# A two-layer diffusion trunk on one core: the seams between ten stages of one kernel are reordered

## The chip, the cores and the metric

The kernel runs on one core of one Trainium2 chip. The metric is the device time of one execution in microseconds (us). The engines of a core are TensorE (PE in the profile; its weight loads are shown apart as PEld), VectorE (DVE), ScalarE (ACT), GpSimd (POOL) and SyncE (SP, which here only issues transfers). Each engine works through its own queue in order, and semaphores make one wait for another. A measured time is the median of several executions; a profiled execution is a single one, with its trace.

## The reference

A trunk of two layers works on 1024 latent tokens and 256 context tokens of width 1024. Every layer modulates its input with a shift and a scale that come from a condition vector, mixes tokens by attention, adds the gated result to the input and normalises it; then it does the same with a feed-forward that has a convolution over three tokens inside. Cut to what matters:

```python
for l in range(DEPTH):                       # 2 layers
    m_lat = split6(silu(c) @ ada_w[l] + ada_b[l])        # shift, scale, gate, twice
    m_ctx = split6(silu(c_ctx) @ ada_w[l] + ada_b[l])
    h_lat, h_ctx = modulate(x_lat, m_lat[0], m_lat[1]), modulate(x_ctx, m_ctx[0], m_ctx[1])
    if l % 2 == 0:   # heads A: global attention, 8 query and 2 key heads, RMS norm and rotary
                     # heads B: neighbourhood attention on a 16x64 grid, 8 heads, learned bias
        y_lat, y_ctx = even_mixer(h_lat, h_ctx, ...)
    else:            # windowed attention (+-128 tokens), 16 query and 2 key heads, sink logits
        y_lat, y_ctx = odd_mixer(h_lat, h_ctx, ...)
    x_lat = layer_norm(ALPHA * x_lat + m_lat[2] * y_lat)
    x_lat = layer_norm(ALPHA * x_lat + m_lat[5] * conv_ffn(modulate(x_lat, m_lat[3], m_lat[4])))
    # layer 0 does the same two steps for x_ctx; layer 1 only uses the context's keys and values
```

`conv_ffn` is `u = h @ w_up` (1024 to 5632), a three-tap convolution along tokens, `silu(g) * a` of the two halves, and `@ w_down` (2816 to 1024). Every latent or context query sees the context keys; all is in 32-bit floats.

## The kernel before

**Precision.** A matrix product is made of three passes: an operand is split into a high part, cast by ACT, and a low part, the difference, made by DVE or POOL, and high x high, low x high and high x low are summed in PSUM (`mm3`, lines 429 to 431; `product`, L1860). So every weight that is loaded costs a cast (L112 or L1832) and a difference (L113 or L1834). In the feed-forwards of the latent tokens the 2x2 blocks of a product are combined with seven multiplications instead of eight; the sums of weight blocks are made on DVE (L1836, L1839; they are called ("s", i) in the code), and the sums of input blocks, T0 to T3, are stored to DRAM (`dT`) and loaded back in `load_T` (hi by ACT, L1889; lo by DVE, L1890).

**Stages in order.** `l0_project` (layer 0's modulated input, query, key and value products, token tile by token tile; then the features of heads B), `attn_ab` (global attention in groups of one token tile and one key head, then neighbourhood attention), `l0_out` (output product, residual, norm), `ffn` (context feed-forward), `ffn2` (latent feed-forward), `l1_project`, `attn_c`, `l1_out`, `ffn7` (latent feed-forward of layer 1). Both output products go through `out_project`.

**What sets the order.** Each engine's order is normally found by a planner from priorities and estimated readiness. In the attention stages and in later parts of `l0_project` the order of TensorE is written by hand (`manual_pe`); in `l1_project` that of TensorE and DVE; in `ffn`, `ffn2` and `ffn7` that of all engines. `out_project` is left to the planner. SP's queue issues most loads, and an issue that waits for something holds back all that stand behind it.

**The places that matter here.**

- *Modulation sums.* `ada_items` walks over the modulation weights still missing in layer 0, in eight jobs of seven steps: loads of `araw`, DVE multiply-adds into `acc` (L228, the first product of a column L224), the split of the result (ACT L325, DVE L326), and a sum over partitions by two matmuls with ones into a PSUM bank `small` (L330, L331), followed by an add on DVE (L332). The matmuls wait in `self.pend` until some tiles have passed. `bg(n)` in `l0_project` advances n steps after each token tile or feature chunk. Steps left over run out in one piece after the second feature product.
- *Global attention.* `groups_a` gives a list of groups (key head, token tile); tiles 8 and 9 are the context. A group's scores (matmul L910) go through a row pass on DVE (L1156 for latent keys, L1173 for context keys: negate and take the minimum), an exponential on ACT (L933), a reciprocal on DVE (L935) and a scaling on POOL (L936); then they are transposed (L1043) and multiplied with the values (L1057). `pipeline` takes units as tuples whose second number says how many slots ahead the scores are issued. `mod_late` (L367 to L370) turns modulation rows into coefficients, at two groups of this stage.
- *Neighbourhood attention.* `slices_b`; the context unit has its scores and its row passes (L1289) for two token tiles in one loop.
- *Output product.* `out_project` loads, for each token tile, x, then y; y is split by ACT (L1457) and POOL (L1458). The first tile's y is ready from before.
- *Context feed-forward.* `ffn` begins with the broadcast of the gate (L159), then the first row of down weights (`row(0)`, L1611). Up weights of part f + 2 are loaded at part f.
- *Latent feed-forward of layer 1.* `build_B1` makes the last token tile's input and the sums; `ffn7` then loads T0 and T1, and after their use T2 and T3 into the same buffers. Each part multiplies W1 with T0 into V, later W4 with T1 into Y, then W5 with T2 into Q (read by L2498, through a copy L2480).
- *Second projection.* `l1_project` scales rows of x by the norm's gain and adds its bias (`scale_rows`, L2627 and L2628), a tile at a time.
- *Windowed attention.* `attn_c`; the row pass is L2887, with a maximum `nm`. At eight of its groups `x_load` fetches a row block of x and scales it with `scale_rows` on DVE.

## Time and profile before

| | before |
|---|---|
| times of three runs | 2835.11, 2832.03, 2835.51 us (median 2835.11) |
| profiled execution | 2826.76 us, span 2825.0 us |
| mean granted clock of TensorE | 0.993 of full speed |
| TensorE busy | 2739.5 us, 97% of the span |
| DVE, ACT, POOL busy | 2155.0 (76%), 1380.8 (49%), 641.9 us (23%) |
| HBM traffic | 161 GB/s over the span |

The profile comes from one execution. A row of waits names the instruction that waited, what released it, and then the total us, how often, and the longest. A row of a timeline has start, duration, engine, line, operation and operands, and in brackets the idle time before it with its releaser. In a window's row the busy time and number of instructions of each engine stand behind the length of the window, then the clock granted to TensorE, the busy share of the DMA engines and the GB/s moved. Matmuls overlap, so the duration of one is longer than its pace.

### The profile page before, as it was taken

To read this page: it belongs to the slowest core of one execution; us is meant where nothing else is said; L and a number is where in the kernel's file an instruction comes from. 1 tells how busy PE (TensorE), PEld (TensorE's weight loads), DVE (VectorE), ACT (ScalarE), POOL (GpSimd) and SP (SyncE) were. 2 spreads that over 40 slices of the span, in tenths; PEclk is the share of its full clock that TensorE was granted. 3 is DMA by queue.
4 is the path that set the end of the run, shared out by engine and by line. 5 is a ranking of instruction groups with operands and counts; after the bars stand their busy time and mean duration, and the time that the engine had idled before them with its cause. 6 is when DMAs were issued, how large, how long until landed. Compare 5 with 4: busy or idle time off the path is not lost.

```text
span 2825.0 us, 45395 instructions
## 1 busy us (share of the span) xinstructions
PE 2739.5 (97%) x16724; PEld 2244.3 (79%) x16724; DVE 2155.0 (76%) x3887; ACT 1380.8 (49%) x2596; POOL 641.9 (23%) x933
## 2 busy tenths in 40 slices
PE   8999899999999999999999999999999999999998
PEld 6887677877788978888888888866678788888887
DVE  4756777776688778888888656677778888888878
ACT  4321355577336645555553345266654555455542
POOL 3601233355440000000001002255543011111002
PEclk9999999999999999999999999999999999999999
DMA  7668601042549653433358525662235455555962
GB/s 272 192 193 284 217 26 35 11 163 91 183 131 275 198 158 110 123 109 117 114 205 291 176 97 165 186 183 90 89 112 168 146 179 175 167 174 200 342 229 97
DMA packets 369350, 457.02 MB, mean 162 GB/s; under 512 B 26008, under 2 KB 265016, under 8 KB 367592
## 3 DMA queue, kind: packets, MB, share of 16 engines
q1 hardware_dynamic: 341512, 369.27, 41.0%
q0 software_dynamic: 24576, 82.89, 8.5%
q8 instruction: 131, 2.15, 0.3%
q10 hardware_dynamic: 3040, 1.97, 0.2%
q14 instruction: 91, 0.75, 0.1%
HBM read 338.11 MB, written 115.93 MB: 161 GB/s over the span
## 4 chain that ended last, share of the span: by engine, by line
PE 74%; issue 9%; DVE 7%; DMA 3%; ACT 3%; POOL 2%; SPq 0%; ACTq 0%; DVEq 0%; POOLq 0%
PE q L1860 8%; PE x L1860 8%; PE y L1860 8%; PE S L910 4%; PE v L1860 4%; PE dy L2544 4%; PE mm L429 4%; PE mm L431 4%; PE mm L430 4%; PE T L1043 3%; PE pv L1057 3%; PE dx L2544 3%; PE d L431 3%; PE d L429 3%; PE d L430 3%
## 5 line engine op out<-in xcount | busy, mean ns | idle before, releaser
L936 POOL TENSOR_SCALAR P<-P,rin 128x640 f32<-128x640 f32 (+3 forms) x288 | 251.1, 877 | 312.6 <-DVE rin L935 285.3
L1834 DVE TENSOR_TENSOR w<-raw,w 128x512 fp32r<-128x512 f32 x308 | 209.9, 695 | 84.3 <-ACT w L1832 84.2
L112 ACT CAST w<-raw 128x512 fp32r<-128x512 f32 x315 | 183.3, 620 | 163.9 <-PE d L431 67.1
L113 DVE TENSOR_TENSOR w<-raw,w 128x512 fp32r<-128x512 f32 x315 | 207.9, 701 | 71.3 <-ACT w L112 69.3
L910 PE MATMUL S<-k,q 64*128 64x256 f32 (+2 forms) x1824 | 199.1, 338 | 20.6 <-DVE nm L2887 8.8
L933 ACT ACTIVATE P<-P,nm 128x641 f32<-128x641 f32 (+4 forms) x208 | 161.5, 778 | 86.8 <-DVE nm L2887 46.0
L1832 ACT CAST w<-raw 128x512 fp32r<-128x512 f32 x308 | 182.2, 620 | 17.2 <-DVE raw L1839 7.5
L910 PEld LDWEIGHTS S<-k,q 64*128 64x128 f32 x1824 | 138.9, 188 | 60.3 <-issue 15.3
L1043 PE MATMUL T<-ident,P 128*128 128x128 f32 x1008 | 133.9, 281 | 5.4 <-POOL P L936 4.9
L429 PE MATMUL d<-w,w 128*128 128x512 f32 x352 | 137.5, 391 | 0.0
L431 PE MATMUL d<-w,w 128*128 128x512 f32 x352 | 137.0, 389 | 0.0
L430 PE MATMUL d<-w,w 128*128 128x512 f32 x352 | 137.0, 389 | 0.0
L1057 PE MATMUL pv<-PT,v 128*64 128x128 f32 x2016 | 131.0, 278 | 4.6 <-ACT PT L923 2.4
L1057 PEld LDWEIGHTS pv<-PT,v 128*64 128x64 f32 x2016 | 108.8, 137 | 28.2 <-issue 13.1
L1043 PEld LDWEIGHTS T<-ident,P 128*128 128x128 f32 x1008 | 109.5, 142 | 24.4 <-issue 14.5
L935 DVE RECIPROCAL rin<-den 128x1 f32<-128x1 f32 x288 | 46.0, 161 | 100.7 <-ACT P L933 97.7
L1860 PE MATMUL q<-T3h,w 128*128 128x512 f32 x352 | 117.1, 394 | 5.7 <-DVE ug L2092 3.1
L2544 PE MATMUL dy<-w,w 128*128 128x512 f32 x528 | 120.8, 390 | 0.2 <-DVE w L113 0.2
L1860 PE MATMUL q<-T2h,w 128*128 128x512 f32 x352 | 115.9, 390 | 2.1 <-ACT q L2480 1.7
L933 ACT ACTIVATE P<-P,mc 128x1280 f32<-128x1280 f32 (+1 forms) x80 | 94.7, 1189 | 44.1 <-DVE mc L1178 41.9
L2544 PEld LDWEIGHTS dy<-w,w 128*128 128x128 f32 x528 | 98.9, 188 | 21.6 <-DVE w L113 0.6
L1860 PE MATMUL v<-T0h,w 128*128 128x512 f32 x352 | 115.5, 389 | 0.0
(465 smaller groups left out, 7786.4 us busy)
## 6 DMA issues: line engine op xcount, KB each, us to landing
raw<-in_up_dram SPq DMA_DIRECT2D x132, 512.0 KB
raw<-in_down_dram SPq DMA_DIRECT2D x59, 512.0 KB
raw<-g SPq DMA_DIRECT2D x44, 512.0 KB
raw<-G SPq DMA_DIRECT2D x38, 512.0 KB
araw<-in_ada_w_dram SPq DMA_DIRECT2D x32, 512.0 KB
raw<-in_w_in_dram SPq DMA_DIRECT2D x28, 512.0 KB
g<-cv POOLq DMA_DIRECT2D x22, 512.0 KB, 3.0
G<-go POOLq DMA_DIRECT2D x44, 256.0 KB, 3.0
```

What stands on the lines that cost most here:

```text
L113: (lo_eng or nc.vector).tensor_sub(lo, s, f32(hi))
L429: nc.tensor.matmul(ps, lh, rh, start=first, stop=False)
L430: nc.tensor.matmul(ps, lh, rl, start=False, stop=False)
L431: nc.tensor.matmul(ps, ll, rh, start=False, stop=last)
L910: self.nc.tensor.matmul(outs[a], q[r, x, qs], k[r, y, ks], start=(i == 0), stop=(i == 2))
L933: nc.scalar.activation(P[:, :m], P[:, :m], AF.Exp, bias=negm, scale=-1.0, accum_out=den)
L936: nc.gpsimd.tensor_scalar(P[:, :n], P[:, :n], rin, 1.0, ALU.mult, ALU.mult)
L1043: nc.tensor.transpose(ps[:, s * 128 : (s + 1) * 128], P[a][:, cols[i + x] : cols[i + x] + 128], self.ident,)
L1057: nc.tensor.matmul(O[a * HD : (a + 1) * HD], v_of(a, vts[i + x]), pT[:, s * 128 : (s + 1) * 128], start=(i + x == 0), stop=(i + x == m - 1 ...
L1834: nc.vector.tensor_sub(half(i, 1), src[i], f32(half(i, 0)))
L1860: nc.tensor.matmul(ps, w[:, a, s], r[b][:, k], start=first and k + i == 0, stop=k == 3 and i == 2, skip_group_check=True,)
L2544: nc.tensor.matmul(banks[q][t], ga[i][:, a, c], wd[i][:, b], start=q < 2 and f + k == 0, stop=f == HF - 1 and k == 2, skip_group_check=True,)
```

## The change

It has ten parts, all of order or placement, in the order of the kernel's stages.

1. The PSUM pool of the modulation sums has two banks instead of one; a pending sum is issued one tile earlier, and more steps are issued per tile.
2. In the global attention a latent group stands between the two context groups; the four heads of a context group share one tile P, and its scores are issued two slots ahead instead of seven.
3. The modulation coefficients made in that stage go from DVE to POOL.
4. The context unit of the neighbourhood attention issues all its scores ahead of its row passes.
5. `out_project` issues the load of the second tile's y ahead of the gate and of x.
6. The first down row and the up weights of part 3 are loaded in the stage before `ffn`, and the row is split there; the gate's broadcast moves into part 4.
7. The weight sum ("s", 1) of the first part of `ffn2` is made at the end of `ffn`.
8. In `ffn7` all four T are staged at once, T1 first, in other buffers; for three of them the first low part is made by POOL, and so is one low part in `build_B1`. Parts with products made ahead take T1's product in front of T0's.
9. `l1_project` scales rows one tile ahead.
10. In `attn_c` the multiply stands behind the row pass of a group's first unit, the add behind the second's.

Two tiles named "pad", 128 bytes per partition each, go. The core of the diff:

```diff
@@ mod_late
+        eng = eng or nc.vector
-                nc.vector.tensor_scalar(s1, ct[:, o + 8 : o + 16], 1.0, None, ALU.add)
-                nc.vector.tensor_mul(ab[:, 0], ct[:, 0:8], s1)
...
+                eng.tensor_scalar(s1, ct[:, o + 8 : o + 16], 1.0, 1.0, ALU.add, ALU.mult)
+                eng.tensor_mul(ab[:, 0], ct[:, 0:8], s1)
...
@@ l0_project
-            if self.pend and self.pend[0][0] > 2:
+            if self.pend and self.pend[0][0] > 1:
...
-                bg(1 if t < 2 else 2)
+                bg(2 if t < 1 else 3)
...
-            banks[0] = e3.enter_context(self.pool("paf", bufs=1, space=PSUM))
+            banks[0] = e3.enter_context(self.pool("paf", bufs=2, space=PSUM))
...
-                    bg(0 if scale and len(n_ev) > 10 else 2 if n > 256 else 1)
+                    bg(0 if scale and len(n_ev) > 10 else 2)
@@ groups_a
-                    for _ in range(4):
-                        P.append(self.t(Pp, [128, TALL], "P"))
+                    if t < NLAT:
+                        P += [self.t(Pp, [128, TALL], "P") for _ in range(4)]
+                    else:
+                        r = self.t(Pp, [128, TALL], "P")
+                        P += [r[:, h * 256 : h * 256 + 256] for h in range(4)]
...
-                        return [(ctx_part, 7, lambda: banks(0) + banks(1), 4, 1)]
+                        return [(ctx_part, 2, lambda: banks(0) + banks(1), 4, 1)]
...
-                group(kv, t, t == NLAT) for kv in range(2) for t in [8, 9] + list(range(NLAT))
+                group(kv, t, t == NLAT) for kv in range(2) for t in [8, 0, 9] + list(range(1, NLAT))
@@ slices_b, context unit, behind the two qk_pair calls
+                for i, x in enumerate(gs):
+                    c = slice(256 + i * 256, 512 + i * 256)
@@ out_project
+        def load_y(t):
+            ys[t] = yh, yl = [self.t(st, [128, KT, 128], n, R, bufs=2) for n in ("yh", "yl")]
+            for q in range(2):
+                s = slice(4 * q, 4 * q + 4)
+                nc.sync.dma_start(f32(yl[:, s]), yv[:, s, t * 128 : (t + 1) * 128])
+
+        load_y(order[1])
         gate_of(order[0])
@@ l0_out, where the first up parts are made
+                r = self.t(self.raw, [128, D], "raw")
+                nc.sync.dma_start(r, io["down"][0][:128])
+                W["r"] = self.up_raws(0, 3)
                 W["u"] = {f: self.ctx_up(pu, W[f], h2c) for f in range(2)}
+                W["d"] = self.split([r[:, :512], r[:, 512:]], 512)
@@ ffn
-            self.bcast(gate, gate_row)
...
-            row(0)
...
                 if f == 4:
+                    self.bcast(gate, gate_row)
...
-            self.early = (part, raws[NP + 1])
+            self.early = (part, self.up_parts(raws[NP + 1]))
+            self.early[1][1]("s", 1)
@@ build_B1
-            nc.vector.tensor_sub(l, s, f32(h))
+            (nc.gpsimd if t == NLAT - 1 else nc.vector).tensor_sub(l, s, f32(h))
@@ ffn7 (staging buffers and load_T changed to fit)
+                for i in range(2):
+                    for m in (1, 0, 2, 3):
+                        make[m].load(i)
...
+                for m in (1, 0, 2, 3):
+                    make[m](0, eng=nc.gpsimd if m != 1 else None)
+                    make[m](1, 2)
...
+                    def first():
+                        self.product(W[1], T[0], V, True)
+                        nc.scalar.copy(u1, cols(V))
+
+                    def second():
+                        self.product(W[4], T[1], Y, False)
+                        nc.scalar.copy(Q, Y)
+
+                    two = (second, first) if p in pre else (first, second)
+                    two[0]()
...
+                    two[1]()
@@ l1_project
-                        load_rows(t + 1)
-                        self.scale_rows(*xs.pop(t), gb["ln_g"], gb["ln_b"])
+                        for u in (0, 1) if t == 0 else (t + 1,):
+                            load_rows(u + 1)
+                            if u < NLAT:
+                                self.scale_rows(*xs.pop(u), gb["ln_g"], gb["ln_b"])
@@ attn_c
-                self.scale_rows(*xs[t], *gb)
+
+            def behind(scores, f):
+                def g():
+                    a, b = scores()
+                    return [
+                        a[:2] + (lambda: (a[2](), f(0))[0],) + a[3:],
+                        b[:2] + (lambda: (b[2](), f(1))[0],) + b[3:],
+                    ]
+                return g
+
+            def x_scale(t, i):
+                x, dr = xs[t]
+                if i == 0:
+                    nc.vector.tensor_mul(x, x, gb[0])
+                else:
+                    nc.vector.tensor_add(x, x, gb[1])
+                    nc.gpsimd.dma_start(dr, x)
...
+                for t, g in enumerate(xg):
+                    gl[g] = gl[g][0], behind(gl[g][1], lambda i, t=t: x_scale(t, i))
```

More of the change, by code (lines that the diff above doesn't have):

```diff
@@ L350, in ada_sum, with mod_late @@
         nc.sync.dma_start(self.d["ada"][l, v, part : part + 1, o : o + W], br)
-    def mod_late(self, tp, pp, lg, lb, mods, tag, bufs=1, bank="small"):
+    def mod_late(self, tp, pp, lg, lb, mods, tag, bufs=1, bank="small", eng=None):
         nc = self.nc
+        eng = eng or nc.vector
         rows = [self.row128(lg), self.row128(lb)]
@@ L1095, in mods @@
                         sp, pt, io["ln_g"][0, i], io["ln_b"][0, i],
-                        [(a[l, v, p], a[l, v, p + 1]) for v in range(2)], tag, 2, "T",
+                        [(a[l, v, p], a[l, v, p + 1]) for v in range(2)], tag, 2, "T", nc.gpsimd,
                     ))
@@ L1451, in out_project @@
             else:
-                yh, yl = (self.t(st, [128, KT, 128], n, R, bufs=2) for n in ("yh", "yl"))
+                if t not in ys:
+                    load_y(t)
+                yh, yl = ys.pop(t)
                 for q in range(2):
@@ L1863, in product, with load_T @@
                 )
-    def load_T(self, tp, stage, dT, m, off):
+    def load_T(self, tp, stage, dT, m, off, late=False):
         nc = self.nc
@@ L1880, in rows, with load, make @@
             return r[:, a - c * n // 2 : b - c * n // 2]
-        for x in part[: 2 if J == 128 else 3]:
-            nc.sync.dma_start(rows(*x), dT[m, :, x[1] : x[2]])
-        def make(*which):
+        def load(i):
+            nc.sync.dma_start(rows(*part[i]), dT[m, :, part[i][1] : part[i][2]])
+        for i in () if late else range(2 if J == 128 else 3):
+            load(i)
+        def make(*which, eng=None):
             for i in which:
@@ L1889, in make @@
                 nc.scalar.copy(hv, r)
-                nc.vector.tensor_sub(lv, r, f32(hv))
+                (eng or nc.vector).tensor_sub(lv, r, f32(hv))
+        make.load = load
         return (h, lo), make
@@ L2038, in ffn2 @@
                         call = lambda what, i: i in (0, 2) or call0(what, i)
+                    elif p == 0:
+                        W2, call0 = raws
+                        call = lambda what, i: (what, i) == ("s", 1) or call0(what, i)
                     elif p + 1 < NP:
@@ L2407, in get_T @@
                 if m in more:
-                    T[m], make[m] = self.load_T(tp, stage(m), dT, m, 0)
+                    T[m], make[m] = self.load_T(tp, stage(m), dT, m, 0, True)
             def make_T(m, *which):
@@ L2428, in ffn7 @@
                 for m in range(4):
-                    if m == 2 and 0 in make:
-                        make_T(0)
-                        make_T(1)
                     get_T(m)
-                    for p in pre if m == 1 else []:
-                        Q = self.t(pu, [128, 512], f"q{p}")
-                        YQ[p] = early["x", p], early["y", p], Q
-                        adds(Q)
+                for i in range(2):
+                    for m in (1, 0, 2, 3):
+                        make[m].load(i)
+                for p in pre:
+                    Q = self.t(pu, [128, 512], f"q{p}")
+                    YQ[p] = early["x", p], early["y", p], Q
+                    adds(Q)
+                for m in (1, 0, 2, 3):
+                    make[m](0, eng=nc.gpsimd if m != 1 else None)
+                    make[m](1, 2)
                 for p in range(NP):
```

47 lines of the change are left out of this document (23 added, 24 removed).

## The prediction

> **What bounds the kernel now.** The first view is the table of busy time by engine.
>
> ```profile
> PE 2739.5 (97%) x16724; PEld 2244.3 (79%) x16724; DVE 2155.0 (76%) x3887; ACT 1380.8 (49%) x2596; POOL 641.9 (23%) x933
> ```
>
> TensorE is busy for 97% of a span of 2825.0 us, so all its waits together are 85.5 us, and nothing but these, or the speed at which it runs, can be won without taking work from it. The change takes no matrix work away. So the second view is TensorE's waits, asked for each seam apart; the rows stand with the steps below. The third is its granted clock, in windows laid over every place where it falls between start-up and the last microseconds; each row has the stretch, its length, the busy time of TensorE, its weight loads, VectorE (DVE), ScalarE (ACT) and GpSimd (POOL), then the clock.
>
> ```profile
> 225.70:232.50 6.80, 4.91 (x38) 3.78 (x36) 3.94 (x7) 0.60 (x1) 0.53 (x1) 1.00 0.89 303
> 232.50:239.30 6.80, 6.47 (x20) 4.09 (x21) 6.66 (x12) 1.41 (x3) 0.53 (x1) 0.50 0.89 288
> 324.70:328.10 3.40, 3.30 (x20) 2.92 (x20) 0.00 (x0) 1.17 (x2) 0.89 (x2) 0.50 0.26 71
> 570.50:573.90 3.40, 3.40 (x26) 3.07 (x23) 1.12 (x5) 1.06 (x4) 1.87 (x5) 0.50 0.34 145
> 853.80:860.60 6.80, 4.74 (x11) 3.43 (x12) 5.05 (x11) 4.40 (x9) 0.77 (x1) 0.50 1.09 345
> 1051.80:1055.20 3.40, 2.86 (x7) 2.31 (x8) 3.37 (x7) 0.00 (x0) 0.00 (x0) 0.51 0.00 0
> 1840.20:1850.40 10.20, 8.96 (x44) 6.87 (x46) 6.31 (x18) 6.07 (x15) 4.05 (x9) 0.50 0.95 321
> ```
>
> The first row is a stretch at full clock for comparison; the six others run at 0.50. At half clock the busy time is twice what it need be, so half of it is lost: 3.2, 1.65, 1.7, 2.4, 1.4 and 4.5 us, 14.9 us in all. Each such stretch follows a wait, and each lies at a seam that the change touches. A step below is therefore worth its wait, and sometimes the clock after it.
>
> **The change part by part.** Gains are positive; each has a value that I take and two ends.
>
> *1, modulation sums in the first projection.*
>
> ```profile
> PE small L330 <- DVE abr L332: 3.0, 2, 2.2
> ```
>
> The second matmul of a sum (L330) waits for the vector add that frees the one PSUM bank (L332). With two banks it does not, and the clock fall behind it (3.2) should go: 2.7 of 3.0 taken, and 3.2. Against it stands the work on DVE. More steps are now issued per token tile, three instead of two.
>
> ```profile
> L228 DVE SCALAR_TENSOR_TENSOR acc<-araw,cs,acc 128x512 f32<-128x512 f32 x10 | 7.3, 750 | 2.4 <-DMA araw<-in_ada_w_dram 2.2
> L326 DVE TENSOR_TENSOR ahl<-acc,ahl 128x512 fp32r<-128x512 f32 x2 | 1.4, 692 | 0.1
> L332 DVE TENSOR_TENSOR abr<-small,abr 1x512 f32<-1x512 f32 x2 | 1.4, 682 | 6.0 <-PE small L331 6.0
> L224 DVE TENSOR_SCALAR acc<-araw,cs 128x512 f32<-128x512 f32 x2 | 1.0, 488 | 0.1
> ```
> ```profile
> 160.00:180.00 20.00, 20.00 (x90) 16.45 (x89) 10.74 (x17) 5.28 (x9) 0.00 (x0) 1.00 0.31 104
> ```
>
> One job of seven steps has 14 multiply-adds, 2 first products, 2 splits and 2 adds: 14 x 0.750 + 2 x (0.488 + 0.692 + 0.682) = 14.2 us of DVE. TensorE runs 90 matmuls in 20.00 us, 0.222 each, so a token tile of 24 takes 5.33 us and seven steps at three per tile 12.4 us. DVE falls back 1.8 us per job; 29 steps in this stage are 4.1 jobs, 7.4 us. Until now it had 6.0 us in these 20 us in which it merely waited for L331, so I expect some of that lag to be swallowed. What is left is late next in the weight splits for the following projection. Cost between 0 and 7.4; taken 3. Net 2.7 + 3.2 - 3 = 2.9 (ends -7.4 to 6.2).
>
> *2, start and middle of the global attention.*
>
> ```profile
> PE small L330 <- DVE rin L935: 3.2, 1, 3.2
> PE T L1043 <- POOL P L936: 2.9, 3, 1.1
> PE S L910 <- DVE P L1173: 1.4, 2, 0.7
> ```
>
> The first row is the tail of the sums, run out in one piece after the projection, behind the softmax on DVE; with more steps per tile the 56 steps end before it: 3.2 and the clock 1.65. The other two (4.3) are context groups standing back to back: little matrix work between two softmaxes. A latent group between them, and the context scores issued two slots ahead instead of seven, gives cover; the transposes still need the same normalisation on POOL, so I take half, 2.1. In the middle, where the second head group starts, the same pattern:
>
> ```profile
> PE T L1043 <- POOL P L936: 2.0, 3, 1.0
> ```
>
> again half, 1.0. Together 8.0 (1.0 to 11.2).
>
> *3, modulation coefficients to GpSimd.*
>
> ```profile
> PE S L910 <- DVE P L1156: 3.5, 2, 1.8
> ```
> ```profile
> 384.97 1.30 DVE L370 TENSOR_TENSOR m1ab<-m1ab,m1c 128x8 f32<-128x8 f32 x2
> ```
>
> Eight tiny DVE operations, the last two shown, which alone take 1.30 us, stand in front of the row passes L1156 for which TensorE then waits 3.5 us. They go to an engine that has nothing to do at that time until its next normalisation, and are needed only by the output stage hundreds of us later. 3.2 (0 to 3.5).
>
> *4, context unit of the neighbourhood attention.*
>
> ```profile
> PE S L910 <- DVE P L1289: 2.9, 5, 1.0
> ```
>
> The second head pair's scores stood behind the first's row passes only in program order; both PSUM tiles exist. 2.4 of 2.9, and half of the 1.7 of clock: 3.2 (0 to 4.6).
>
> *5, y rows ahead in both output projections.*
>
> ```profile
> PE o L429 <- ACT yh L1457: 2.8, 2, 1.5
> PE o L431 <- POOL yl L1458: 2.7, 4, 0.9
> ```
>
> Two waits of ACT's cast, one per layer, and two of the four on POOL's difference, 1.4 of 2.7 if they are alike, are the second tile's y, loaded behind a gate broadcast and x on the sync queue. The two y transfers go in front of three others; x and the gate move back by two issues, and are needed one tile of matmuls later. 3.0 of 4.2 (0 to 4.2): the transfer's own time stays.
>
> *6, first down row of the context feed-forward.*
>
> ```profile
> PE d L429 <- ACT w L112: 4.3, 1, 4.3
> ```
> ```profile
> 849.49 0.34 SPq L159 DMA_DIRECT2D gate<-ada  x1
> 849.88 0.50 SPq L1611 DMA_DIRECT2D raw<-in_down_dram  x1
> ```
> ```profile
> 855.19 1.14 ACT L112 CAST w<-raw 128x512 fp32r<-128x512 f32 x2 [3.44 <-DMA raw<-in_down_dram]
> ```
>
> The row is issued behind the gate's broadcast, which itself waits for an earlier store; the cast that waits for its landing starts at 855.19, and the first down matmul follows at once. In the change the row is issued in the stage before, and its split is made there. Its landing then precedes its use by more than the 5.3 us from issue (849.88) to cast. The two casts (1.14) and two differences move into a stage in which the tile before is normalised. 4.0 and the clock 2.4: 6.4 (4.3 to 6.7). This is the surest step.
>
> *7, the first sum of the next feed-forward's weights, ahead.*
>
> ```profile
> PE q L1860 <- DVE ug L2092: 3.1, 1, 3.1
> PE d L429 <- ACT w L112: 1.6, 1, 1.6
> PE d L430 <- DVE w L113: 0.7, 2, 0.5
> ```
>
> The add for part 1 sat among the last context tiles in DVE's queue, waiting for its raw weights; the change puts it after the last down product. The 3.1 is the other end of the same delayed chain, through the store of the last input sum and its reload, of which only the DVE part moves. Half: 2.7, and half the clock 0.7: 3.4 (0 to 6.8).
>
> *8, the Strassen-like feed-forward of layer 1 starts with T1.*
>
> ```profile
> PE q L1860 <- ACT q L2480: 1.7, 2, 1.0
> PE q L1860 <- DVE ug L2498: 1.7, 1, 1.7
> PE v L1860 <- DVE T0l L1890: 1.0, 1, 1.0
> ```
>
> T1's product now goes first and all four inputs are staged at once, so these 4.4 could go. But four differences go from DVE to GpSimd: three of 128x1024 and one of 128x512.
>
> ```profile
> L1424 POOL TENSOR_TENSOR w<-P,w x3: 1282/1282/2379, 695.3 to 2050.1; 128x512 fp32r<-128x512 f32 x2, 128x1024 fp32r<-128x1024 f32 x1
> ```
> ```profile
> 806.52 3.56 DVE L1478 SCALAR_TENSOR_TENSOR x<-x,hst 128x512 f32<-128x512 f32 x1
> ```
> ```profile
> 807.00 2.52 POOL L1458 TENSOR_TENSOR yl<-yl,yh 128x512 fp32r<-128x512 f32 x2
> ```
>
> The first row prices them: 2.38 us for the large form, 1.28 for the small. The other two show what happens to a two-input DVE operation meanwhile: one of a shape that takes 0.69 alone (L326 above) stood 3.56 us, until both GpSimd operations had ended. Here 3 x 2.38 + 1.28 = 8.4 us of GpSimd work run while DVE must make T1's low parts for the first product. In the worst case these start about 7.5 us late and two clock windows fall (3.4): -11. In the best they slip in between: 4.4. I take -3, nearer to the row. The Trainium skill ("SBUF — State Buffer", section "Who interferes with whom") states it as a rule: the two engines share one port pair, an exclusive lock that blocks a DVE instruction with two SBUF inputs for the whole of a GpSimd instruction that reads SBUF; the trace agrees (3.56 us), and by the rule alone this step is a loss.
>
> *9, row scaling one tile ahead in the second projection.*
>
> ```profile
> PE S L910 <- DVE nm L2887: 3.8, 2, 2.6
> PE S L910 <- issue: 1.5, 1, 1.5
> ```
>
> Two DVE passes of the last tile leave the queue in front of L2887, but the chain through the transposed last q, its store and reload stays. 2.0 of 5.3, and a third of the clock, 1.5: 3.5 (0 to 9.8). At the first tile two scales stand together; the four PSUM banks of that stage hide it.
>
> *10, x scaling behind the row passes in the windowed attention.*
>
> ```profile
> PE S L910 <- DVE nm L2887: 5.0, 8, 1.0
> ```
>
> Eight of ten places at which L2887 stood behind an x multiply that waited for its load. Now it stands ahead of it: 4.2 (0 to 5.0).
>
> The sum: 2.9 + 8.0 + 3.2 + 3.2 + 3.0 + 6.4 + 3.4 - 3 + 3.5 + 4.2 = 34.8 us. For what becomes last at each of ten seams when the present wait is gone I take off 0.3 us each, an estimate from the smallest rows above (0.7 in two parts): 31.8. The profiled execution took 2826.76 us (span 2825.0); it becomes 2795.0. The median shown is 2835.11, 8.35 above that execution, so on its footing 2803.3.
>
> **The rivals.**
>
> *A, the waits only move.* TensorE waits as long for the next engine in the chain: DVE is at 76% and the softmax chains at steps 2, 4 and 9 are not shortened. For it: the waits have different releasers in one place (step 2's three). Against: steps 3, 6 and 10 take an instruction out of a queue. Half the gain: 2819.
>
> *B, the clock does not come back.* The waits go, but 10.3 us of clock in the sum stay lost, since shifted seams fall into other windows: gain 21.5, 2813.6. For it: the fall at 570.5 followed waits of at most 1.0, and the one at 232.5 a stretch with 4.91 of 6.80 us busy. The Trainium skill ("TensorE: Matmul & The Clock Gate", "What's actually happening") has a free-running window of 3413 ns and a fall after an idle one; the lengths here, 3.4 and its multiples, agree, the need for a whole idle window doesn't.
>
> *C, GpSimd holds DVE at step 8 throughout.* -11 in place of -3: gain 23.8, 2811.3.
>
> *D, slower: DVE paces the first projection.* At three steps a tile DVE needs 14.2 x 3 / 7 = 6.1 us. If it also waits for the sums' weights, which must now arrive faster, TensorE follows it, since each sum's matmul waits for DVE's split. The L228 row has 2.2 us of such waiting in 3.75 tiles; were it 2.4 per tile, a tile would take 8.5 us, 3.2 over, times ten tiles 32, and two clock windows 3.4. The rest gives 34.8 - 2.9 - 3 = 28.9, so the time would be 2841.6; it decides from about 1.8 us of waiting per tile. Against it: that row shows a third of this, 0.6.
>
> *E, it does not do what it says.* Outside the feed-forwards and the second projection only TensorE's order is written by hand; a planner may put the other engines' moved work back. Then steps 6 to 9 alone count, 10.3 - 3 = 7.3: 2828, and 2836 if step 8 is at its worst.
>
> **How the numbers follow.** Forecast 0.44, A 0.17, B 0.10, C 0.10, D 0.06, E 0.13. A measurement of this kernel can tell about 0.2%, 5.7 us, from no change. Faster than that are the forecast, A, B, C and a part of E (0.04), less a little for their tails: 0.84. Within it lies most of E: 0.08. Slower: D and the tails, 0.08. The terms' half spans (6.8, 5.1, 1.8, 2.3, 2.1, 1.2, 3.4, 7.7, 4.9, 2.5) are independent; the root of their squares' sum is 13.7, so the forecast's own range is 2790 to 2817. It is carried up to 2825, past A, leaving out D and most of E, and down to 2788.
>
> **What would show it.** Right: no wait of TensorE for the first down row (step 6) and full clock after it; no row L332 or L1156 of any size; the x rows gone from L2887's waits; total TensorE idle near 60 us instead of 85.5, and half clock in two stretches at most. Wrong: DVE above 95% with TensorE waiting for L326 or L113 between 150 and 200 us (step 1, D); DVE operations of 2 to 8 us beside GpSimd differences at the start of the last feed-forward, with TensorE waiting for T1's low part (step 8, C); the same totals under new names (A).

## The result and the profile after

The changed kernel takes 2815.95 us (median; 2811.69 to 2817.18) against 2834.82 us: 18.9 us less, a ratio of 0.9933 with a 95% interval of 0.9915 to 0.995. The forecast was 2803, its range 2788 to 2825. The direction was right and the size 13 us too good.

The page of the changed kernel, engine by engine:

```profile
PE 2739.8 (97%) x16724; PEld 2245.4 (80%) x16724; DVE 2147.6 (76%) x3867; ACT 1381.5 (49%) x2596; POOL 657.7 (23%) x953
```

With a span of 2815.3 us TensorE now waits 75.5 us, against 85.5 before. So the waits pay for 10 us of the 18.9. The forecast's sum had 24.5 us of waits and 10.3 of clock, less 3 for what comes late next. TensorE's waits in the changed kernel, the rows that matter (lines have moved by 1 to 60; L911 is the old L910, L1044 the old L1043, L2947 the old L2887, L1879 the old L1860):

```profile
PE q L1879 <- DVE ug L2539: 7.1, 5, 2.7
...
PE pv L1018 <- ACT PT L924: 4.8, 12, 0.6
PE T L1044 <- POOL P L937: 4.7, 3, 2.6
PE T L1044 <- ACT PT L918: 4.6, 2, 2.3
PE S L911 <- DVE nm L2947: 4.4, 8, 1.0
...
PE tr L1740 <- ACT x L400: 2.6, 1, 2.6
...
PE o L432 <- POOL yl L1474: 1.1, 2, 0.7
```

The rows of L1156 (step 3), of the y cast L1457 and of the first down matmul's cast (steps 5 and 6) are gone. Of L2887's old 8.8 us 4.4 are left. But four rows are new or have grown: the transposes wait 4.6 us for ACT's copies (L918), the last feed-forward waits 7.1 us for L2539 (the old L2498, 2.5 us), the values' product in the windowed attention waits 4.8 us for ACT (3.0 before), and the transposes of x in the context's norm wait 2.6 us for ACT (0.7 before).

Stage windows show where that left the time. Three stages of the kernel before, then of the changed one: both attentions of layer 0, the output product with the context feed-forward, and everything from the second output product on. The two stages between the second and the third row are left out.

```profile
316.60:711.00 394.40, 370.83 (x4086) 301.77 (x4086) 282.20 (x846) 242.03 (x495) 171.05 (x186) 0.99 0.23 75
711.00:1031.20 320.20, 309.69 (x1885) 275.32 (x1881) 252.40 (x421) 160.71 (x339) 65.81 (x76) 0.99 0.66 200
2079.50:2825.00 745.50, 727.51 (x3230) 598.94 (x3226) 630.36 (x842) 357.43 (x573) 113.22 (x180) 1.00 0.56 187
```

```profile
315.50:708.30 392.80, 372.40 (x4082) 302.87 (x4082) 273.41 (x826) 241.07 (x494) 173.46 (x201) 0.98 0.23 76
708.30:1020.90 312.60, 307.71 (x1883) 275.58 (x1880) 251.79 (x420) 160.23 (x339) 65.56 (x76) 0.99 0.68 204
2066.50:2815.30 748.80, 729.24 (x3230) 599.96 (x3226) 632.75 (x838) 358.12 (x573) 127.41 (x184) 0.99 0.56 186
```

A row's length less its busy time is what TensorE waited. The second of these stages gave 7.6 us, of which 5.6 are waits (10.5 to 4.9). The attentions, where steps 2 to 4 promised 14, gave 1.6 us. The last stage lost 3.3. By all stages:

| stage | before: length / waits | after: length / waits |
|---|---|---|
| first projection (step 1) | 316.6 / 14.7 | 315.5 / 14.7 |
| attentions of layer 0 (2, 3, 4) | 394.4 / 23.6 | 392.8 / 20.4 |
| output, context feed-forward (5, 6) | 320.2 / 10.5 | 312.6 / 4.9 |
| latent feed-forward, second projection (7, 9) | 803.1 / 4.3 | 803.0 / 3.8 |
| windowed attention (9, 10) | 245.2 / 14.4 | 242.6 / 12.2 |
| second output, last feed-forward (5, 8) | 745.5 / 18.0 | 748.8 / 19.6 |

The two profiled executions differ by only 9.7 us of span, half of the 18.9. The first experiment is about that.

### The profile page after: what moved, and what is told of

Read it like the earlier page. It is cut to its first block, busy times and chain, and to the rows that moved or that the text cites. A ratio compares the mean times of both kernels' runs of the same rounds, so it can differ in the third digit from the quotient of the medians.

```text
span 2815.3 us, 45394 instructions
## 1 busy us (share of the span) xinstructions
PE 2739.8 (97%) x16724; PEld 2245.4 (80%) x16724; DVE 2147.6 (76%) x3867; ACT 1381.5 (49%) x2596; POOL 657.7 (23%) x953
## 4 chain that ended last, share of the span: by engine, by line
PE 70%; issue 10%; DVE 9%; DMA 4%; ACT 3%; POOL 2%; SPq 0%; ACTq 0%; DVEq 0%; POOLq 0%
PE q L1879 7%; PE x L1879 7%; PE y L1879 6%; PE S L911 5%; PE dy L2585 4%; PE T L1044 4%; PE pv L1058 4%; PE mm L430 3%; PE v L1879 3%; PE mm L432 3%; PE mm L431 3%; PE dx L2585 3%; PE d L431 3%; PE d L432 3%; PE d L430 3%
## 5 line engine op out<-in xcount | busy, mean ns | idle before, releaser
L113 DVE TENSOR_TENSOR w<-raw,w 128x512 fp32r<-128x512 f32 x315 | 206.0, 695 | 69.5 <-ACT w L112 67.5
L911 PE MATMUL S<-k,q 64*128 64x256 f32 (+2 forms) x1824 | 198.4, 340 | 11.4 <-DVE nm L2947 4.4
L934 ACT ACTIVATE P<-P,nm 128x641 f32<-128x641 f32 (+4 forms) x208 | 161.4, 777 | 86.1 <-DVE nm L2947 46.4
L911 PEld LDWEIGHTS S<-k,q 64*128 64x128 f32 x1824 | 139.3, 190 | 49.6 <-issue 16.0
L1044 PE MATMUL T<-ident,P 128*128 128x128 f32 x1008 | 136.7, 283 | 12.0 <-POOL P L937 4.7
L1044 PEld LDWEIGHTS T<-ident,P 128*128 128x128 f32 x1008 | 110.5, 143 | 32.2 <-issue 17.9
L1879 PE MATMUL q<-T3h,w 128*128 128x512 f32 x352 | 118.7, 399 | 9.1 <-DVE ug L2539 7.1
L1879 PE MATMUL q<-T2h,w 128*128 128x512 f32 x352 | 115.8, 390 | 0.9 <-ACT q L2101 0.9
L1879 PE MATMUL y<-T1h,w 128*128 128x512 f32 x352 | 115.5, 389 | 0.0
```

Source lines behind the costliest of these rows:

```text
L113: (lo_eng or nc.vector).tensor_sub(lo, s, f32(hi))
L911: self.nc.tensor.matmul(outs[a], q[r, x, qs], k[r, y, ks], start=(i == 0), stop=(i == 2))
L934: nc.scalar.activation(P[:, :m], P[:, :m], AF.Exp, bias=negm, scale=-1.0, accum_out=den)
L1044: nc.tensor.transpose(ps[:, s * 128 : (s + 1) * 128], P[a][:, cols[i + x] : cols[i + x] + 128], self.ident,)
L1879: nc.tensor.matmul(ps, w[:, a, s], r[b][:, k], start=first and k + i == 0, stop=k == 3 and i == 2, skip_group_check=True,)
```

## The experiments

All ratios are to the kernel before, timed in the same sitting. A ratio's 95% interval is about 0.0015 to each side, 4 us, so single parts are judged by their waits in the trace and by the time together.

### What the profile of before was worth

No edit: the kernel before, profiled a second time.

> The kernel before, unchanged, for a second profile of it. Theory: the profile that the prediction was made from (2826.76 us) shows an unusually quick execution, and an ordinary one takes 2831 to 2836 us with more of TensorE's waits or of its half-clock stretches (idle above 85.5 us, or over 34 us at half clock) at places that are the same otherwise. Rival: profiled executions are always about 8 us below the timed ones; then this profile again shows 2825 to 2828 us while the times stay at 2832 to 2836.

Its profiled execution took 2832.59 us with a span of 2830.8; its ratio was 0.9994 (0.9985 to 1.0003). TensorE's waits are the same, 86.1 us (2830.8 less 2744.7 busy). What differs is the granted clock. Over the 23 executions of this program in that sitting it ran from 0.988 to 0.992, and the time went with it: 2839.2 us on average at 0.988, 2832.5 at 0.992. The execution on which the prediction was built had 0.993. It was a lucky one: the second profile lies 2.3 us under the median of its runs and not 8. So the theory holds and the rival, an offset of all profiles, falls.

Part of where the luck lay can be read in windows of 3.4 us, laid on the grid on which the half-clock stretches of each trace begin. First the execution behind the prediction, at step 3's first wait (3.5 us for two):

```profile
386.10:389.50 3.40, 1.79 (x15) 1.24 (x17) 2.46 (x12) 0.14 (x1) 0.09 (x1) 1.00 0.00 0
389.50:392.90 3.40, 3.40 (x38) 2.89 (x35) 3.27 (x8) 1.82 (x3) 0.00 (x0) 1.00 0.02 5
```

Then the second execution of the same program, at the same wait:

```profile
387.20:390.60 3.40, 1.73 (x13) 1.21 (x15) 2.48 (x12) 0.21 (x1) 0.15 (x1) 1.00 0.00 0
390.60:394.00 3.40, 3.40 (x24) 3.07 (x23) 2.31 (x6) 0.52 (x1) 0.00 (x0) 0.50 0.02 5
```

The same wait, of about 1.7 us, left TensorE busy for 1.79 us of one window there, and for 1.73 here. There the next window kept full clock; here it ran at 0.50, and 24 matmuls ran in it in place of 38. The grid's start differs from execution to execution, so whether a wait costs clock is in part a matter of chance. The changed kernel's four executions had 0.992 to 0.995, 0.9935 on average, against 0.990 for the 23 of before. At the 1.7 us per thousandth that the 23 show, an estimate from clocks given to a thousandth, that is about 6 us: the waits' 10 and the clock's 6 come near the 18.9. The remaining 3 us I cannot place; they lie within the interval, which is 5 us to each side.

### Part 2, and which piece of it

All of part 2 is put back in the changed kernel. The edit, cut at the dots:

```diff
-                    if t < NLAT:
-                        P += [self.t(Pp, [128, TALL], "P") for _ in range(4)]
-                    else:
-                        r = self.t(Pp, [128, TALL], "P")
-                        P += [r[:, h * 256 : h * 256 + 256] for h in range(4)]
+                    for _ in range(4):
+                        P.append(self.t(Pp, [128, TALL], "P"))
...
-                        return [(ctx_part, 2, lambda: banks(0) + banks(1), 4, 1)]
+                        return [(ctx_part, 7, lambda: banks(0) + banks(1), 4, 1)]
...
-                group(kv, t, t == NLAT) for kv in range(2) for t in [8, 0, 9] + list(range(1, NLAT))
+                group(kv, t, t == NLAT) for kv in range(2) for t in [8, 9] + list(range(NLAT))
```

> The changed kernel with part 2 undone (context groups back to back, four P tiles, seven slots ahead). Theory: in the changed kernel part 2 has only moved the waits of the global attention (about 11.2 us before, 13.5 after, new ones of 2.3 us each at 362.9 and 487.9 us behind ACT's copies) and lost clock with them (one half-clock stretch of 3.4 us before, four after), so undoing it gains 3 to 7 us on 2815.95: 2809 to 2813, with no wait of over 2 us of the transposes on ACT. Rival: the end of the modulation sums' tail is owed to part 2; then it loses 2 to 6 us: 2818 to 2822.

Measured 0.9898 (0.9883 to 0.9913), 2809.55 us: by the ratios part 2 had cost about 10 us, and with both intervals between 3 and 16, an estimate. The two attentions took 386.4 us instead of 392.8. The waits that it had added stand in ACT's queue; the changed kernel there, ACT and then TensorE:

```profile
359.58 1.36 ACT L934 ACTIVATE P<-P,mc 128x1280 f32<-128x1280 f32 x1 [3.81 <-DVE mc L1182]
...
360.94 1.35 ACT L934 ACTIVATE P<-P,mc 128x1280 f32<-128x1280 f32 x1
...
362.29 1.05 ACT L918 COPY PT<-T 128x512 f32<-128x512 f32 x2
```

```profile
362.90 0.47 PE L1044 MATMUL T<-ident,P 128*128 128x128 f32 x1 [2.32 <-ACT PT L918]
```

A copy L918 that frees a bank for the next transposes stands behind two exponentials of 1.36 us. These wait for row passes that start late; that the context group between the latent ones makes them late is my reading. The next run tests whether the order is the cause. TensorE stood for 2.32 us, and again at 487.9 in the second half; both windows of clock that follow ran at 0.50.

Then the order alone was put back, with the shared tile and the two slots kept:

```diff
-                group(kv, t, t == NLAT) for kv in range(2) for t in [8, 0, 9] + list(range(1, NLAT))
+                group(kv, t, t == NLAT) for kv in range(2) for t in [8, 9] + list(range(NLAT))
```

> The changed kernel with only the order of the groups in part 2 put back (both context groups first); the shared tile P and the two slots stay. Theory: the waits of 2.3 us on ACT's copies come from the latent group between the context groups, whose exponentials stand ahead of the copies in ACT's queue, so this kernel has none and is as fast as the one with part 2 undone: ratio 0.989 to 0.991. Rival: the two slots instead of seven are the cause; then the waits stay and the ratio is that of the changed kernel, 0.993.

Measured 0.9902 (0.9885 to 0.9919), 2806.43 us. The theory holds: the order is the loss. Neither wait of 2.3 us on ACT's copies is left, and the waits of both attentions fall from 20.4 us to 14.4. Waits of this kernel at the start of the stage, then in its middle:

```profile
PE T L1044 <- POOL P L937: 4.3, 3, 2.6
```

```profile
PE T L1044 <- POOL P L937: 0.5, 1, 0.5
```

In the middle 0.9 us is left, two rows of 0.2 with it, of the 3.2 that the kernel before had there, and of the 3.3 with all of part 2 undone. So the slots and the shared tile are worth 2.4 us of waits there, which the time does not show (0.9902 against 0.9898), and the order loses more than that. At the start nothing helped: with part 1 in, POOL's scaling ends the longest wait, 2.6 us, in either order.

### Part 8: two engines that hold each other

```diff
-                    make[m](0, eng=nc.gpsimd if m != 1 else None)
+                    make[m](0)
-            (nc.gpsimd if t == NLAT - 1 else nc.vector).tensor_sub(l, s, f32(h))
+            nc.vector.tensor_sub(l, s, f32(h))
```

> The changed kernel with the four low parts of part 8 made by VectorE as before; the staging and T1 in front of T0 stay. Theory: the two engines hold each other up (POOL's 1.3 us difference took 6.41, three DVE differences of 0.69 took 2.84 to 2.88), so without POOL the waits at the start of the last feed-forward (7.05 us) shrink to 2 to 4 and its half-clock stretch goes: 2810 to 2814. Rival: DVE is simply full there, and with 4.3 us more of its own work the waits for L2539's add grow by about 4 us: 2818 to 2821.

Measured 0.9903 (0.9885 to 0.992), 2810.82 us, 5 us under the changed kernel by the medians and 8 by the ratios, though the intervals overlap. The traces decide. In the changed kernel POOL's queue at that place reads:

```profile
2170.23 6.41 POOL L1797 TENSOR_TENSOR h3lbl<-hst,h3lbh 128x512 fp32r<-128x512 f32 x1 [3.18 <-DVE h3lbh L1796]
2176.60 2.36 POOL L1912 TENSOR_TENSOR T0l<-ua,T0h 128x1024 fp32r<-128x1024 f32 x1
2178.93 2.85 POOL L1912 TENSOR_TENSOR T2l<-cv,T2h 128x1024 fp32r<-128x1024 f32 x1
```

and DVE's differences of 128x512 beside it, from the last one that ran at its own pace:

```profile
2174.80 0.69 DVE L1912 TENSOR_TENSOR T0l<-w,T0h 128x512 fp32r<-128x512 f32 x1
2176.67 2.84 DVE L1912 TENSOR_TENSOR T2l<-ua,T2h 128x512 fp32r<-128x512 f32 x1 [1.19 <-POOL h3lbl L1797]
2179.44 2.88 DVE L1912 TENSOR_TENSOR T2l<-w,T2h 128x512 fp32r<-128x512 f32 x1
```

The first POOL difference, priced at 1.28, took 6.41 us: it began beside a row of eight DVE operations without a gap, the last of which is the first row above, and ended 1.2 us after that row did. From then on the roles change. Each DVE difference, 0.69 us when alone, ended about 0.55 us after the POOL operation that had begun ahead of it, and so took 2.84 and 2.88. What TensorE waited for in this stretch, in the changed kernel and then with VectorE's low parts:

```profile
PE q L1879 <- DVE ug L2539: 4.6, 2, 2.7
PE v L1879 <- POOL T0l L1912: 1.6, 1, 1.6
PE q L1879 <- DVE T2l L1912: 0.4, 1, 0.4
PE y L1879 <- DVE T1l L1912: 0.4, 1, 0.4
```

```profile
PE q L1879 <- DVE ug L2539: 2.7, 1, 2.7
PE y L1879 <- DVE T1l L1912: 1.0, 1, 1.0
```

7.0 against 3.7 us, with more work on DVE. The rival (DVE is full, more work hurts) falls. The same four rows, 7.0 to 7.1 us, stand in the traces with part 2 undone and with its order put back, so they are no accident of one execution.

Part 8 undone altogether (all its lines as before):

> The changed kernel with part 8 undone altogether. Theory: part 8 as a whole turned 4.4 us of waits into 7.05 and added one half-clock stretch (1.7), so undoing it gains about 4: 2810 to 2814, and the waits are those of before (1.0, 1.05, 0.7 and 1.7). Rival: T1 in front is a gain that POOL's part eats; then this kernel is 2 to 4 us slower than the one with VectorE's low parts.

Measured 0.9909 (0.9894 to 0.9924), 2811.15 us, the same as with VectorE's low parts. T1 in front and the early staging bring nothing that these runs can measure; POOL's part is the loss.

### Both undone, and the later split

Parts 2 and 8 both as before:

> The changed kernel with parts 2 and 8 both undone. Theory: the two losses lie in different stages and add, about 8 and 5 us on the changed kernel: ratio to before 0.987 to 0.990, waits of TensorE below 62 us. Rival: what undoing either gained was mostly the clock, which falls differently in each execution, so both together give no more than one: 0.990 to 0.992.

Measured 0.99 (0.9884 to 0.9916), 2806.04 us. By the ratio that is no better than part 2 undone alone (0.9898) and hardly better than part 8 (0.9909), as the rival had it. The waits are 70.3 us, against 73.2 without part 2 alone and 75.5 in the changed kernel; the theory had put them below 62. The interval holds both readings; the last pair below speaks for adding.

In the same kernel, the first down row split behind the gate again:

```diff
-                W["d"] = self.split([r[:, :512], r[:, 512:]], 512)
+                W["d"] = r
...
-            u, rows, raws, gts, wd, gb, make = W["u"], {}, {3: W["r"]}, {}, {0: W["d"]}, [], {}
+            u, rows, raws, gts, wd, gb, make = W["u"], {0: W["d"]}, {3: W["r"]}, {}, {}, [], {}
...
-                if 0 < c < NP:
+                if c < NP:
```

> Parts 2 and 8 undone, and in part 6 the first down row is still loaded early but split where it was before, behind the first gate. Theory: in the changed kernel the early split (two differences on DVE) stands ahead of the last context norm and costs the wait of the transposes on x (2.6 us in the changed kernel, 0.7 before), and the up products behind it another 1.0 to 1.3; with the late split these shrink to 1.5 together and the down wait of 4.3 stays away: 1 to 3 us below the kernel without parts 2 and 8. Rival: the split's lateness makes the down matmul wait again by 1 to 2 us, and nothing is won.

Measured 0.9905 (0.9888 to 0.9923): nothing won. My reading of the 2.6 us for the transposes on x was wrong at the root. The kernel without the edit shows there:

```profile
PE u L432 <- DVE w L113: 1.3, 1, 1.3
PE d L430 <- ACT hst L1743: 0.9, 1, 0.9
PE tr L1737 <- ACT x L400: 0.7, 1, 0.7
```

so the early split alone does not make the 2.6. Of the nine traces with the early split, five have 0.7 there and four have 2.0 to 2.6. It comes and goes in programs that have the same code in this stage: 0.7 and 2.4 in the two kernels of the last pair below. What differs can be seen ahead of it in ACT's queue, in the changed kernel and then in the one of the next section, whose wait is 0.7:

```profile
833.91 1.15 ACT L112 CAST w<-raw 128x512 fp32r<-128x512 f32 x2 [10.36 <-DMA raw<-in_up_dram]
```

```profile
832.47 1.14 ACT L112 CAST w<-raw 128x512 fp32r<-128x512 f32 x2 [8.52 <-DMA raw<-in_up_dram]
```

The cast of an up weight waited 1.8 us longer for its transfer, and the norm's scaling stands behind this cast. All nine traces agree: five casts waited 8.5 us, and the transposes then 0.7; four waited 9.8 to 10.4, and the transposes 2.0 to 2.6. Why the transfer is late in some executions the traces do not show.

### Part 1 undone

One bank, the sums later, fewer steps per tile, as before.

> The changed kernel with part 1 undone (one bank, sums later, fewer steps per tile). Theory: the wait for the bank's add (2.2 us near 230), the tail of sums after the second feature product (about 3 us near 320) and the clock behind them come back: 4 to 8 us slower than the changed kernel, ratio 0.995 to 0.996. Rival: with one bank the steps cost no more than the loss of DVE's reserve that three steps per tile bring; then the ratio stays at 0.993.

Measured 0.9936 (0.992 to 0.9951), as the rival had it. Its waits in the projection and at the tail behind it, then those of the changed kernel:

```profile
PE small L330 <- DVE abr L332: 5.8, 4, 3.2
PE T L1044 <- DVE abr L332: 0.9, 1, 0.9
```

```profile
PE T L1044 <- POOL P L937: 2.6, 1, 2.6
PE small L330 <- DVE abr L332: 1.6, 2, 0.9
```

The sums' own waits go from 5.8 us, the tail's 3.2 among them, to 1.6. But the first transposes of the attention, which had 0.9 to wait behind that tail, now wait 2.6 for POOL's scaling. With the rows not shown, 7.2 us became 5.6, and the time does not show even that.

### Part 6 undone, and three parts alone

The row, its split and the up weights of part 3 leave `l0_out`, and the broadcast and the row stand at the start of `ffn` again. The edit, cut at the dots:

```diff
-                r = self.t(self.raw, [128, D], "raw")
-                nc.sync.dma_start(r, io["down"][0][:128])
-                W["r"] = self.up_raws(0, 3)
                 W["u"] = {f: self.ctx_up(pu, W[f], h2c) for f in range(2)}
-                W["d"] = self.split([r[:, :512], r[:, 512:]], 512)
...
+            self.bcast(gate, gate_row)
...
+            row(0)
...
-                    self.bcast(gate, gate_row)
```

> The changed kernel with part 6 undone. Theory: the down wait of 4.3 to 4.5 us comes back with two half-clock windows, and the new waits of 0.9 and 1.3 us go: 4 to 6 us slower than the changed kernel, ratio 0.995. Rival: the new waits and the clock they cost eat most of it: under 2 us, ratio 0.9935 to 0.994.

Measured 0.9932 (0.9917 to 0.9946): no loss that could be measured. The surest step of the forecast was worth nothing that the time shows. This trace has 79.6 us of waits, 4.1 more than the changed kernel's, but 2.5 of these lie in the windowed attention, which the edit does not touch: a total of waits from one trace is uncertain by a few us. Then parts 3, 5 and 10 alone, on the kernel before:

> The kernel before with parts 3, 5 and 10 alone, those that take an instruction or a transfer out of a queue in front of one that TensorE waits for. Theory: these keep what the trace of the changed kernel shows of them, 3.5 + 4.3 + 2 us of waits, and the clock behind two waits of 1.7: 9 to 13 us, ratio 0.9955 to 0.997. Rival: each of their waits is followed by the next engine's; then under 5 us, 0.998 to 1.0.

Measured 0.9939 (0.9924 to 0.9954), 2819.15 us: 16 us faster than the kernel before, which these runs cannot tell from what all ten parts give, and more than either expectation had. Its waits came to 73.1 us (2818.1 less 2745.0 busy), 12.4 under those of before, and its clock to 0.9935 on average. Its sync queue shows something about part 6:

```profile
825.61 0.91 SPq L159 DMA_DIRECT2D gate<-ada  x1
826.58 0.49 SPq L1622 DMA_DIRECT2D raw<-in_down_dram  x1
```

The gate's broadcast is issued at 825.61 and the first down row at 826.58; in the kernel before they stood at 849.49 and 849.88. This kernel has no line of part 6. In the kernel before, the sync queue's own waits hold this row:

```profile
SPq L159 <- DMA x<-x: 16.3, 1, 16.3
```

The broadcast waited 16.3 us for a store of x. What has changed is the order in which the output stage allocates its tiles: part 5 allocates the y tiles ahead of x. In the kernel before, the feed-forward's gate lies over a buffer of x, and so waits until x is stored; with part 5 y tiles lie there, which are free early. Both programs' addresses show it. So with part 5 the row comes early enough without part 6. But that is no gain of 4.3 us. The waits at this place in the changed kernel with part 6 undone:

```profile
PE d L431 <- DVE w L113: 2.1, 1, 2.1
PE tr L1737 <- ACT x L400: 1.4, 1, 1.4
PE d L430 <- ACT w L112: 0.7, 1, 0.7
```

The cast's wait is down from 4.3 to 0.7, and 2.8 us have come in its place: 2.1 for the row's low part, made by DVE, and 0.7 more than before for x. In sum it is 4.2 us where the kernel before had 5.0 (4.3 and 0.7). With part 6 it is 3.6 in the changed kernel's trace and 2.9 in the rows of the kernel without parts 2 and 8 above; over the nine traces it runs from 2.9 to 4.7, since the wait on x comes and goes. The up products then wait for their weights' low part. So part 6 is worth at most 1.3 us of waits, and nothing that the time shows.

The kernel with parts 3, 5 and 10 alone also shows part 10 by itself. TensorE's waits in the windowed attention, before and then here:

```profile
PE S L910 <- DVE nm L2887: 5.0, 8, 1.0
PE pv L1017 <- ACT PT L923: 3.0, 8, 0.6
```

```profile
PE pv L1018 <- ACT PT L924: 5.4, 13, 0.6
PE S L911 <- DVE nm L2915: 2.4, 7, 0.4
```

L2887's waits go from 5.0 to 2.4 us, and those of the values' product, for ACT's copies, from 3.0 to 5.4. Together 8.0 and 7.8: the wait moved to the next engine, and nothing was won. In the changed kernel the two rows have 7.5 us in this stretch.

### The two corrections together

The order of part 2 put back, and part 8's low parts on VectorE:

> The changed kernel with the group order of part 2 put back and all low parts of part 8 on VectorE. Theory: the two losses of the change are the order (about 9 us) and the engines' mutual hold-up in part 8 (about 3 us of waits), and they add where they are waits: TensorE's waits come to 53 to 56 us, ratio 0.987 to 0.9895. Rival: as with parts 2 and 8 undone together, the second step is lost in the clock: 0.990 and no difference to the order put back alone.

Measured 0.9878 (0.9862 to 0.9895), 2802.38 us. With part 8 undone instead:

> The changed kernel with the group order of part 2 put back and part 8 undone. Theory: staging all four inputs at once and T1 in front bring under 1 us (waits of 4.4 us against 3.7), so this one is within 0.1% of the kernel with the low parts on VectorE. Rival: loads that come earlier help the first parts as well, and this one is 2 to 4 us slower.

Measured 0.9877 (0.9863 to 0.9892), 2802.72 us. Both are about 33 us faster than the kernel before and by ratio about 16 faster than the changed kernel. The attentions took 384.3 us in the first of these, the last stage 745.4. With the order alone put back it was 0.9902, so the second correction adds, at least by the middle of the intervals. Its trace bears out less: TensorE's waits in the last stage go from 17.8 us with the order alone to 16.4, and all waits only from 67.1 to 66.6, where the theory had 53 to 56. As expected, the staging of part 8 makes no difference.

## Why the prediction was right or wrong

**Right.** What follows is told in waits; parts 4, 7 and 9 were neither run alone nor undone, so what they are worth in time is not shown. *Step 3*: 3.5 us of waits were there and all are gone; forecast 3.2. *Step 4*: all the waits in the neighbourhood attention went from 8.3 to 6.1 us, 2.2 for a forecast of 2.4; its clock fall came back at another place. *Step 7*: 5.8 us around its seam became 3.1, 2.7 as forecast, though the half was a guess; the half-clock window behind it stayed. *Step 9*: 5.3 became 3.2, 2.1 for a forecast of 2.0; but the half-clock stretch of 10.2 us behind it stayed, of which the sum had 1.5. *Step 8*, taken as a loss of 3: 4.4 us became 7.0, and one clock window fell. The sign came from the row of 3.56 us, in which DVE stood beside GpSimd. The mechanism is that row's, but its first act went the other way round: DVE held GpSimd for 5 us. So T1's low parts, which I had put up to 7.5 us late, came 0.4 late, and the price fell on T0, T2 and the adds behind them. The rule of the Trainium skill ("SBUF — State Buffer", "Who interferes with whom") is that whichever of the two issues first gets the shared ports for its whole instruction and the other fully blocks. The trace agrees that DVE can block GpSimd too (6.41 us for a 1.28 us operation), but the block lasted over eight DVE instructions and not one. Who issued first cannot be read from the start times: in the row of 3.56 us DVE's operation has the earlier one (806.52 against 807.00) and yet stood until GpSimd had ended.

**Wrong: step 2 (8.0).** Of its 8.0 only 3.1 stand for the lines of part 2; the other 4.9, the tail of the sums and its clock, hang on the steps per tile of part 1. The 3.1 were counted as a gain because the context groups stood back to back. The step that failed is that a "latent group between them" gives cover. A latent group's exponentials stand in ACT's queue ahead of the copies that free the transposes' banks, two waits of 2.3 us and their clock. I had looked at what TensorE would have to do, and not at what would be queued behind what on ACT. Part 2 as a whole cost about 10 us of time (0.9933 against 0.9898), so these 3.1 were off by 13, as much as the whole miss.

**Wrong: step 6 (6.4).** "This is the surest step" was said of a wait, and the wait did go; what failed is that all of it was counted as won. Behind the late row stood DVE's splits, of the row itself or of the up weights, which come late next: 1.0 to 2.2 us of waits for L113 in every version, beside those on x. And I read that the gate "itself waits for an earlier store" without asking why a broadcast into a new tile should. The reason was where the tile lay, and part 5 had already moved it. *Step 5* itself, put at 3.0, won 4.4: the rows L1457 and L1458 have 1.1 of 5.5 left.

**Wrong: step 10 (4.2).** It won 0.2. The instruction did leave the queue in front of L2887, but the chain goes on through ACT's copies, and these came late next. That is rival A, which I had argued against for this very step: "steps 3, 6 and 10 take an instruction out of a queue".

**Step 1 (2.9, and the 4.9 of the tail in step 2).** The feared lag of DVE did not come (no wait on the weight splits of the projection above 0.3 us), and the gain did not either, within what can be measured (0.9936 without part 1, 0.9933 with it): the tail that was to be finished early gave its place to POOL's scaling. Rival D stayed far away.

**The rivals.** A holds for steps 10, 6 and half of step 1. It was priced as a half of the sum; weighed seam by seam, with the next engine in each chain, it would have come nearer. B does not hold on average: the clock rose from 0.990 to 0.9935, about 6 us of the 10.3 in the sum. The pair of profiles hides this, since the one before was quick and the one after is the slowest of its four runs. That offset of 8.35 us I had carried over in full, as if it belonged to the profile and not to the execution. E does not hold: the rows of step 5 are gone and those of L2887 have halved, and these orders were the planner's to undo. Of the signs that the prediction named, the rows of L1156 and of the first down matmul's cast went as it said, but TensorE waited 75.5 us and not near 60, and half clock stands in nine stretches ahead of the last microseconds and not in two. That the total missed by no more than 13 is partly luck: part 2 was 13 too good, and step 1 with the tail (7.8), step 6 (6.4) and step 10 (4.2) were all but empty. Against that stand parts 3, 5 and 10, which alone gave 16 us for a forecast of 10.4, and the clock of ordinary executions, which had more to give back than the quick one showed.

## What to carry to other kernels

When a step is moved to give TensorE cover, write down for every other engine which instructions then stand ahead of the ones that free TensorE's banks; a late copy behind two exponentials costs as much as the wait that was cured. A wait that ends is worth only the distance to the next one at the same place, which one run with the part alone shows. And before DVE's work goes to GpSimd, look at what the two will run side by side: here the tiny operations of step 3, moved to a time when GpSimd was free, won 3.5 us, and the differences of step 8 beside DVE's own lost 3.3.

## What the runs showed of the hardware

The clock's price for a wait depends on the execution. In each of the fourteen traces all half-clock stretches begin on one grid of 3.41 us whose start differs from run to run, and a window with TensorE busy for 1.73 us of 3.40 was followed by a half-clock one, one with 1.79 was not. It is no sharp bound on busy time either: with part 2 undone a window at 1034.3 had 1.52 us busy and the next kept full clock. The same program so ranged from 2830.44 to 2840.88 us in 23 executions; its two traces, of 2826.76 and 2832.59 us, have the same waits, 85.5 and 86.1 us.

A transfer into a fresh tile can wait for the last reader of another tile that lay in its memory: 16.3 us for the gate, which went when the tiles were allocated in another order. It is issued 24 us earlier then (825.61 for 849.49); the rest is that the issue ahead of it came earlier (825.13 for 832.68).

The hold between DVE and GpSimd works both ways. DVE's eight operations without a gap held one GpSimd difference until they were through: 6.41 us for one of 1.28. In the other direction each DVE difference of 0.69 stood until the GpSimd operation ahead of it had ended, 2.84 to 2.88 us, and the next GpSimd operation became 0.5 us longer (2.85 for 2.36).
